# Longer rows for the loads, three stores for four, and a later release of the first store, in a streaming add and GELU kernel

## The chip, the cores and the metric

One core of one Trainium2 chip (each batch of runs on one chip, not always the same). The metric is the device time of one execution in microseconds (us). The kernel before took 121.92 us, median of three runs (121.77 to 122.04).

## The reference

Two float32 arrays of 1024 x 4096 are added, and the tanh form of GELU is taken of the sum:

```python
def reference(x, y):
    z = x + y
    return (0.5 * z * (1 + np.tanh(np.sqrt(2 / np.pi) * (z + 0.044715 * z ** 3)))).astype(np.float32)
```

That is 33.55 MB to load and 16.78 MB to store, with a dozen operations per element.

## The kernel before

Each of the 128 partitions owns 8 rows, so a flat row of 32,768 values. The work is cut into 16 chunks of 2048 columns. GELU is computed as z times a sigmoid: POOL adds x and y (DVE does it for chunk 0), ACT squares into PSUM, DVE does a multiply-add there, ACT takes the sigmoid, and DVE multiplies PSUM by z back into SBUF. All transfers are issued by SP, in this order, to one DMA queue; x is loaded straight into the buffer `zt`, which also takes the result; y has two buffers of 8192 columns, so the third block of y waits for the adds of the first. The stores wait for the multiplies of their chunks, and the first store for that of chunk `FIRST` as well.

```python
    YS = 8192
    CH = 2048
    PS = 2
    loads = [2048, 6144, 8192, 8192, 8192]
    FIRST = 8
    stores = [16384, 8192, 4096, 4096]
    # ... cut ...
    by_pool = set(range(1, C))
    # ... cut ...
    def store(i):
        a, b = sr[i]
        ins = nc.sync.dma_start(out=ov[:, a:b], in_=zt[:, a:b])
        if i == 0:
            tc.add_manual_dep(
                ins.ins,
                muls[FIRST].name,
                mybir.DependencyInfo(mybir.DependencyClass.Sync, mybir.DependencyReason.DATA),
                reason="the stores join the queue when the last load is nearly done",
            )
    # ... cut ...
    def mul(c):
        a, b = cr[c]
        muls[c] = nc.vector.tensor_mul(out=zt[:, a:b], in0=wt[c], in1=zt[:, a:b]).ins
```

## Time and profile before

| | before |
|---|---|
| time, three runs | 121.77 to 122.04 us |
| span of the profiled run | 119.75 us |
| DMA queue, share of 16 engines' span | 98.6% |
| DVE, POOL, ACT busy | 62%, 56%, 51% |
| first packet starts, last packet ends | 1.03 us, 119.19 us |
| first store issued | 76.44 us |

The queue's row is the one to read first: the DMA engines are busy for 98.6% of the span and the busiest compute engine for 62%, so the question is what is in the queue. The prediction shows the lines.

A *packet* is one record of the DMA's work in the trace (start, duration, bytes); here it is one row of a transfer in one partition. The *turn* is where a DMA engine passes from its last load packet to its first store packet. The *stall* is what load packets before the turn lasted over the median of their size (1213 ns for 32 KB), summed and divided by the 16 engines. Where single engines are told of, their chains were put together from the packets' times, since the records carry no engine number.

### The profile page before, as it was taken

The numbers are of one execution on the slowest core, as the hardware profiler recorded it, in microseconds if no ns is written. First come the engines' busy times: TensorE is split into PE (matmuls) and PEld (weight loads), VectorE is DVE, ScalarE is ACT, GpSimd is POOL, SyncE is SP. The second block draws the span as 40 slices with busy tenths as digits, with TensorE's granted clock in tenths as the row PEclk, the third lists the DMA queues.
The fourth block names the chain that finished last, engine by engine and source line by source line (L and its number), as shares of the span: only waits on it lengthen the run. The fifth ranks groups of instructions, "written<-read, shape, count | busy, mean of one in ns | idle before, by whom it ended". The sixth has DMA issues, their size and how long they took to land.

```text
span 119.8 us, 174 instructions
## 1 busy us (share of the span) xinstructions
DVE 73.7 (62%) x34; ACT 61.0 (51%) x34; POOL 67.5 (56%) x19
## 2 busy tenths in 40 slices
DVE  0053600004999970749999949999993999990000
ACT  4006000009779706197797668888819879800000
POOL 0000000699980199999869999939999990000000
DMA  6999999989898999989898989998899889999996
GB/s 186 421 487 402 476 435 394 514 361 493 383 493 383 438 438 394 482 361 514 350 525 350 525 350 493 383 525 350 350 613 438 350 350 427 449 405 405 427 432 257
DMA packets 2016, 50.33 MB, mean 420 GB/s; under 512 B 224, under 2 KB 224, under 8 KB 224
## 3 DMA queue, kind: packets, MB, share of 16 engines
q1 hardware_dynamic: 2016, 50.33, 98.6%
HBM read 33.55 MB, written 16.78 MB: 420 GB/s over the span
## 4 chain that ended last, share of the span: by engine, by line
DMA 50%; POOL 26%; POOLq 4%; DVE 4%; DVEq 2%; ACT 2%; SPq 1%; issue 0%
DMA y<-in_y_dram 50%; POOL z L145 26%; POOLq L215 4%; DVE w L156 2%; DVEq L215 2%; DVE z L165 2%; ACT w L150 2%; SPq L121 1%; SPq L128 1%; POOLq L145 0%
## 5 line engine op out<-in xcount | busy, mean ns | idle before, releaser
L145 POOL TENSOR_TENSOR z<-z,y 128x2048 f32<-128x2048 f32 x15 | 67.3, 4519 | 31.1 <-DMA y<-in_y_dram 31.1
L156 DVE SCALAR_TENSOR_TENSOR w<-w,z 128x2048 f32<-128x2048 f32 x16 | 36.7, 2296 | 26.4 <-ACT w L150 26.1
L150 ACT ACTIVATE w<-z 128x2048 f32<-128x2048 f32 x16 | 30.1, 1882 | 38.3 <-POOL z L145 29.3
L165 DVE TENSOR_TENSOR z<-w,z 128x2048 f32<-128x2048 f32 x16 | 35.8, 2281 | 0.0
L161 ACT ACTIVATE w<-w 128x2048 f32<-128x2048 f32 x16 | 29.7, 1855 | 4.4 <-DVE w L156 4.4
L145 DVE TENSOR_TENSOR z<-z,y 128x2048 f32<-128x2048 f32 x1 | 2.3, 2293 | 6.1 <-DMA y<-in_y_dram 6.1
L200 ACT ACT_TABLE_LOAD x1 | 1.3, 1283 | 1.3 <-PEq L232 1.3
L199 DVE MEMSET one<- 128x1 f32 x1 | 0.1, 59 | 1.3 <-PEq L232 1.3
L232 POOL MEMSET const-float32-0.0<- 128x1 f32 x1 | 0.1, 98 | 0.2 <-issue 0.2
L200 ACT ACTIVATE one<-one 128x1 f32<-128x1 f32 x1 | 0.2, 203 | 0.0
L232 POOL MEMSET const-bfloat16-1.0<- 128x1 bf16 x1 | 0.1, 101 | 0.0
L232 POOL MEMSET const-uint8-127<- 128x1 uint8 x1 | 0.1, 101 | 0.0
L232 POOL MEMSET const-float32-1.0<- 128x1 f32 x1 | 0.1, 98 | 0.0
## 6 DMA issues: line engine op xcount, KB each, us to landing
z<-in_x_dram SPq DMA_DIRECT2D x3, 4096.0 KB, 34.6
y<-in_y_dram SPq DMA_DIRECT2D x3, 4096.0 KB, 25.3
out_dram<-z SPq DMA_DIRECT2D x1, 4096.0 KB, 22.2
out_dram<-z SPq DMA_DIRECT2D x2, 2048.0 KB, 14.1
z<-in_x_dram SPq DMA_DIRECT2D x1, 3072.0 KB, 13.4
y<-in_y_dram SPq DMA_DIRECT2D x1, 3072.0 KB, 20.3
z<-in_x_dram SPq DMA_DIRECT2D x1, 1024.0 KB, 4.9
y<-in_y_dram SPq DMA_DIRECT2D x1, 1024.0 KB, 6.9
```

What stands on the lines that cost most here:

```text
L121: nc.sync.dma_start(out=zt[:, a:b], in_=xv[:, a:b])
L128: nc.sync.dma_start(out=yt[s][:, o : o + b - a], in_=yv[:, a:b])
L145: eng.tensor_add(out=zt[:, a:b], in0=zt[:, a:b], in1=yt[s][:, o : o + b - a])
L150: nc.scalar.activation(out=wt[c], in_=zt[:, a:b], func=act.Square, scale=root)
L156: nc.vector.scalar_tensor_tensor(out=wt[c], in0=wt[c], scalar=c1, in1=zt[:, a:b], op0=alu.add, op1=alu.mult)
L161: nc.scalar.activation(out=wt[c], in_=wt[c], func=act.Sigmoid)
L165: muls[c] = nc.vector.tensor_mul(out=zt[:, a:b], in0=wt[c], in1=zt[:, a:b]).ins
L199: nc.vector.memset(one, 0.0)
L200: nc.scalar.activation(out=one, in_=one, func=act.Sigmoid)
L215: tc.compile()
L232: nc = _bacc.Bacc("TRN2", target_bir_lowering=False, num_devices=1)
```

## The change

Fewer and longer transfers: eight loads of 32 KB rows in place of ten with 8, 24 and 32 KB; three stores in place of four. The first store is also issued later: it waits for the first half of chunk 9's multiply, not for all of chunk 8's.

```diff
-    loads = [2048, 6144, 8192, 8192, 8192]
-    FIRST = 8
-    stores = [16384, 8192, 4096, 4096]
+    loads = [8192, 8192, 8192, 8192]
+    FIRST = 9
+    stores = [16384, 10240, 6144]
@@
-        muls[c] = nc.vector.tensor_mul(out=zt[:, a:b], in0=wt[c], in1=zt[:, a:b]).ins
+        parts = 2 if c == FIRST else 1
+        n = (b - a) // parts
+        for o in range(0, b - a, n):
+            ins = nc.vector.tensor_mul(
+                out=zt[:, a + o : a + o + n],
+                in0=wt[c][:, o : o + n],
+                in1=zt[:, a + o : a + o + n],
+            )
+            muls.setdefault(c, ins.ins)
```

## The prediction

Where the text below told of the hardware what no trace or run of this case shows, the passage is cut and the place marked. The sum runs 121.92 - 0.23 - 0.1 = 121.6 us (121.59). These numbers stand as estimates:

- the gain of 0.1 us at the start, out of the 0.66 us of excess measured there;
- that DVE's and POOL's first adds, ready together, would run one after the other, so that POOL's would come later by the length of DVE's (2293 ns). The trace before does not show it, since its DVE add ran alone. Rival 1 is the opposite order: POOL's three adds first, DVE's after them;
- the first store at 77.4 us. From the trace alone: half of a multiply of 2.28 us from 76.33 gives 77.47, less the 0.2 us of earlier landings some 77.3;
- the 0.45 us after which the store's descriptors "should reach the engines": it is read off the start of the dent (76.44 to 76.89 us) alone, for the records hold packets and no descriptors. So is the latency of a first store in rival 3, read off the dent's 1.9 us.

> **What bounds the kernel now.** I read the page from the top: engine shares, the row of DMA slices, the queue, then the waits and the chain.
>
> ```profile
> span 119.8 us, 174 instructions
> DVE 73.7 (62%) x34; ACT 61.0 (51%) x34; POOL 67.5 (56%) x19
> ...
> q1 hardware_dynamic: 2016, 50.33, 98.6%
> HBM read 33.55 MB, written 16.78 MB: 420 GB/s over the span
> ```
>
> No compute engine is busy for two thirds of the span; the one DMA queue is busy for 98.6% of it. So the question is what the 16 DMA engines do in 119.75 us. Next the DMA in four stretches (columns: stretch and length, then DVE, ACT, POOL busy, clock, DMA share, GB/s):
>
> ```profile
> 0.00:3.00 3.00, 0.06 (x1) 1.49 (x2) 0.20 (x4) 1.00 0.67 188
> 3.00:76.00 73.00, 44.34 (x20) 37.04 (x20) 46.39 (x11) 1.00 1.01 436
> 76.00:80.00 4.00, 4.00 (x3) 3.03 (x3) 2.94 (x1) 1.00 0.99 369
> 80.00:119.75 39.75, 25.29 (x12) 19.46 (x11) 17.95 (x4) 1.00 0.96 414
> ```
>
> From 3 to 76 us the queue runs flat at 436 GB/s. (A packet's bytes count where it starts, so short windows swing.) It loses at the two ends and in a dent at 76 to 80 us, where the first store joins. The chain of waits says 50% "DMA y" and 26% POOL, and the DMA issues waited 46.4 us for the multiplies; but [...] the 98.6% says that the queue was full. The timeline dates the issues:
>
> ```profile
> 7.47 2.29 DVE L145 TENSOR_TENSOR z<-z,y 128x2048 f32<-128x2048 f32 x1 [6.08 <-DMA y<-in_y_dram]
> ...
> 22.12 13.45 POOL L145 TENSOR_TENSOR z<-z,y 128x2048 f32<-128x2048 f32 x3 [21.69 <-DMA y<-in_y_dram]
> ...
> 48.01 2.30 DVE L156 SCALAR_TENSOR_TENSOR w<-w,z 128x2048 f32<-128x2048 f32 x1 [3.81 <-ACT w L150]
> ...
> 74.13 4.48 DVE L165 TENSOR_TENSOR z<-w,z 128x2048 f32<-128x2048 f32 x2
> ...
> 76.44 31.41 SPq L132 DMA_DIRECT2D out_dram<-z  x4
> ```
>
> The two multiplies from 74.13 are those of chunks 8 and 9 (each 2.28 us); chunk 8's ends at 76.41 and releases the first store at 76.44.
>
> The trace keeps a record of each packet (start, duration, bytes); one row of a transfer is one packet. Median durations: 309 ns for 8 KB, 611 for 16 KB, 912 for 24 KB, 1213 for 32 KB, 2418 for 64 KB, 9 for the 4-byte packet that each engine ends a transfer with. From 8 to 64 KB that is 2109 ns for 57,344 bytes: 0.03678 ns per byte, or 27.19 GB/s per engine, and about 8 ns on top per packet. Now the sum for one of the 16 engines (8 rows of each transfer):
> - first packet at 1.03 us
> - packets at their medians: 16 of 8 KB 4.94, 16 of 24 KB 14.59, 56 of 32 KB 67.93, 8 of 64 KB 19.34, 16 of 16 KB 9.78, 14 end packets 0.13: 116.71 us
> - excess over the medians 1.34 us: 0.66 in packets that start between 1 and 2 us, 0.53 in those from 76 to 80 us, 0.15 scattered
> - last packet's end (119.19) to the end of the span: 0.56 us
>
> Sum 119.64 of 119.75 us. The measured time, 121.92, is 2.17 us more than the span. Nothing but bytes, packet ends, these excesses and the two fixed ends is in the time.
>
> [...] the one DVE add with two SBUF inputs ran alone at 7.47, and the others read one input from PSUM, beside which POOL's adds stay at 4493 to 4541 ns.
>
> **The change, part by part.**
> Fewer packets. The four small loads (8 and 24 KB rows) become two of 32 KB rows; the stores of 32, 16 and 16 KB rows become 40 and 24 KB. Per engine: 64 of 32 KB at 1213 = 77.63; 8 of 64 KB 19.34; 8 of 40 KB, by the line above 1514 each (an estimate), 12.11; 8 of 24 KB 7.30; 11 end packets 0.10. Sum 116.48 us against 116.71: **0.23 us saved**. All of it is on the path, since the queue is the path.
>
> Start. The first packet should still start near 1.03 us. The 0.66 us of excess there sits on the first packet or two of each engine. [...] I count a gain of 0.1, with 0 to 0.4 possible.
>
> The first add. The DVE add of chunk 0 now waits for all of y's first block, as POOL's add of chunk 1 does: both become ready at about 21.8 instead of 7.4 and 22.0. [...] In the trace DVE starts 0.10 us after the landing (7.37 to 7.47), POOL 0.14 us after (21.98 to 22.12), so DVE should win. Then POOL's three adds come 2.3 us later (end 37.9, not 35.57), y's third block is issued at 37.9 rather than 35.60, and the compute of block 0 ends some 2.3 us later. Neither is on the path: x's third block occupies the queue until 50.6, and DVE waited 3.81 us before its instruction at 48.01, which absorbs the shift. Cost 0. Without contention the chain keeps its times too, because before, too, chunk 0's second half waited for chunk 1 at 26.65.
>
> First store. [...] The store is issued at about 77.4, some 1.0 us later. The loads' last packets ended at 79.6 to 80.5; without the dent and with fewer packets they would end at about 78.9 to 79.7. The dent began 0.45 us after the issue (packets from 76.89), so the stores' descriptors should reach the engines at 77.85, still a packet ahead of the end: no bubble. The dent itself I take as the cost of the first store reaching the engines, and keep at 0.53, give or take 0.3.
>
> Later stores. 40 KB rows need the multiply of chunk 12, which ended at 96.3 by the chain; store 0 keeps the queue until 99.3 or later. 24 KB rows need chunk 15 (107.5); store 1 lasts until about 111.5. Margins 3 and 4 us: hidden.
>
> Split multiply: one more DVE instruction[...], on an engine with 38% idle: 0.
>
> Sum: 121.92 - 0.23 - 0.1 = **121.6 us**.
>
> **Rivals.**
> 1. The DVE add starves. [...] add 0 runs at 35.3 to 37.6, block 0 ends at 57.5 instead of 44.2, and with DVE working pairs of chunks in 9.0 us back to back, half of chunk 9 is done at 83.2. The queue runs dry from about 80 to 83.7: about 3.7 us, some 125.4 us. [...] against it: DVE's 0.04 us lead. I give it 5 to 6%.
> 2. The later store removes the dent, because it is caused by store and loads in flight together: 0.5 us less, 121.1. For it: packets are slow only there; against: 1 us later they still overlap.
> 3. The later store is too late: first-store latency falls into an empty queue. 0.3 to 0.6 us more: about 122.0. The dent's 1.9 us from 76.9 to 78.8 suggests that a first store takes time to get going.
>
> **Range and chances.** Rivals 2 and 3 are half a microsecond either side, and before's own three runs span 121.77 to 122.04. So 121.1 to 122.0 should hold it 8 times in 10. Faster by 2% is 119.5, below 1.03 + 116.48 + 0.56 + 2.17 = 120.24, which has no excess at all: 1%. Slower by 2% needs rival 1: 5%.
>
> **What would show it.** Right: 1584 packets, the queue again at 98% or more, a first store issued near 77.4, a dent of about 0.5 us just after it, store packets following loads without a gap, POOL's first adds later by 2.3 us with DVE's add at 21.9 unchanged. Wrong: DVE's add of chunk 0 lasting or starting far later than 22 and the first store after 80 (rival 1); a DMA gap at 79 to 81 us (rival 3); no slow packets there (rival 2); a first-packet excess far from 0.66 us.

## The result and the profile after

The changed kernel took **121.11 us** (median of six runs, 120.99 to 121.43), against 121.80 for the kernel before on the same chip (121.49 to 122.04, six runs). The ratio is 0.9947, with a 95% interval of 0.9929 to 0.9965. All ratios here are the mean time of one kernel's fast runs over that of the other's of the same rounds, so they are not quite the ratios of the medians. By the 2% rule that is "same"; the interval nevertheless excludes 1. The predicted 121.6 was 0.5 us too high.

The page of the changed kernel answers the four lines shown of before:

```profile
span 118.9 us, 170 instructions
DVE 73.7 (62%) x35; ACT 61.0 (51%) x34; POOL 69.7 (59%) x19
...
q1 hardware_dynamic: 1584, 50.33, 98.6%
HBM read 33.55 MB, written 16.78 MB: 423 GB/s over the span
```

It has 1584 packets and the same 98.6%: the queue is still the bound, and only POOL's busy time moved, by 2.2 us. Its DMA by stretches (columns as in the prediction):

```profile
0.00:3.00 3.00, 0.06 (x1) 1.49 (x2) 0.20 (x4) 1.00 0.81 262
3.00:76.00 73.00, 44.57 (x20) 37.15 (x20) 48.80 (x11) 1.00 1.01 435
76.00:80.00 4.00, 4.00 (x4) 3.16 (x2) 2.69 (x1) 1.00 1.22 524
```

The flat part is unchanged (435 against 436 GB/s). The dent is gone: 524 GB/s at 76 to 80 us, against 369. (Bytes count where a packet starts, and here the first 64 KB packets start inside the stretch. The packet records say it without that distortion: the load packets of before between 76 and 80 us had 0.53 us of excess per engine, those of after 0.00.) The timeline of the changed kernel:

```profile
21.84 2.29 DVE L145 TENSOR_TENSOR z<-z,y 128x2048 f32<-128x2048 f32 x1 [20.44 <-DMA y<-in_y_dram]
21.88 15.58 POOL L145 TENSOR_TENSOR z<-z,y 128x2048 f32<-128x2048 f32 x3 [21.44 <-DMA y<-in_y_dram]
...
47.78 2.30 DVE L156 SCALAR_TENSOR_TENSOR w<-w,z 128x2048 f32<-128x2048 f32 x1 [1.69 <-ACT w L150]
...
77.33 29.77 SPq L132 DMA_DIRECT2D out_dram<-z  x3
```

DVE's add and POOL's first add start 0.04 us apart, DVE first. DVE's takes its usual 2.29 us; POOL's three adds take 15.58 us, not 13.45. One group line of each kernel (POOL's adds: shortest, median, longest in ns) shows that a single instruction carries it, first before, then after:

```profile
L145 POOL TENSOR_TENSOR z<-z,y x15: 4493/4518/4541, 22.1 to 94.3; 128x2048 f32<-128x2048 f32 x15
```

```profile
L145 POOL TENSOR_TENSOR z<-z,y x15: 4508/4520/6622, 21.9 to 93.6; 128x2048 f32<-128x2048 f32 x15
```

POOL's first add lasted 2.1 us longer than its usual 4.5. DVE's idle time before its instruction near 48 us shrank from 3.81 to 1.69 us, which is where those 2.1 us ended.

Where the 0.84 us between the two profiled spans went, by the packet records: the 16 engines finished at 118.81 us on average before, and at 118.10 after, 0.71 less. Of this 0.53 is the stall, 0.06 the start (0.66 to 0.60), and 0.12 the rest, mostly the packets saved. The span waits for the slowest engine, and the stall had hit the engines unequally (0.11 to 0.83 us each): the last engine finished 0.38 us behind the mean before, and 0.16 after, 0.22 less. Against it the time from the last packet to the end of the span grew from 0.56 to 0.65. In all 0.71 + 0.22 - 0.09 = 0.84.

So most of the gain is the vanished stall, and the prediction had kept it. Did the later release remove it, or the rows, or chance?

### The profile page after: what moved, and what is told of

The parts are those of the page before. It is cut to its first block, busy times and chain, and to the rows that moved or that the text cites. A ratio compares the mean times of both kernels' runs of the same rounds, so it can differ in the third digit from the quotient of the medians.

```text
span 118.9 us, 170 instructions
## 1 busy us (share of the span) xinstructions
DVE 73.7 (62%) x35; ACT 61.0 (51%) x34; POOL 69.7 (59%) x19
## 2 busy tenths in 40 slices
DMA packets 1584, 50.33 MB, mean 423 GB/s; under 512 B 176, under 2 KB 176, under 8 KB 176
## 3 DMA queue, kind: packets, MB, share of 16 engines
q1 hardware_dynamic: 1584, 50.33, 98.6%
## 4 chain that ended last, share of the span: by engine, by line
DMA 51%; POOL 26%; POOLq 4%; DVE 4%; DVEq 2%; ACT 2%; issue 0%; SPq 0%
DMA y<-in_y_dram 51%; POOL z L145 26%; POOLq L223 4%; DVE w L156 2%; DVEq L223 2%; DVE z L168 2%; ACT w L150 2%; SPq L121 0%; POOLq L145 0%
## 5 line engine op out<-in xcount | busy, mean ns | idle before, releaser
L145 POOL TENSOR_TENSOR z<-z,y 128x2048 f32<-128x2048 f32 x15 | 69.4, 4661 | 28.2 <-DMA y<-in_y_dram 28.2
L168 DVE TENSOR_TENSOR z<-w,z 128x2048 f32<-128x2048 f32 (+1 forms) x17 | 35.9, 2155 | 0.0
L145 DVE TENSOR_TENSOR z<-z,y 128x2048 f32<-128x2048 f32 x1 | 2.3, 2292 | 20.4 <-DMA y<-in_y_dram 20.4
```

Of the source, the lines that this page charges most:

```text
L145: eng.tensor_add(out=zt[:, a:b], in0=zt[:, a:b], in1=yt[s][:, o : o + b - a])
L168: ins = nc.vector.tensor_mul(out=zt[:, a + o : a + o + n], in0=wt[c][:, o : o + n], in1=zt[:, a + o : a + o + n],)
```

## The experiments

Theory A: the stall comes from the first store joining the queue too far ahead of the turn; as I first put it, the stall was to come at the moment of joining. Rival B: it belonged to the old rows, or was chance. Rival C: it falls where the queue turns, however early the store joined. Rivals D and E are about how often it is paid: once, by the first store of the program (D), or at every turn (E). All twelve runs gave correct results; each has a profile. Each time is the median of six executions (e7: four), and a stall is that of the one profiled. The kernel before was timed in each batch.

| run | first store issued, us | stall 76-80 us, us | median, us (range) | ratio to before |
|---|---|---|---|---|
| before, first batch | 76.44 | 0.53 | 121.80 (121.49-122.04) | 1 |
| changed kernel | 77.33 | 0.00 | 121.11 (120.99-121.43) | 0.9947 |
| e1: changed, FIRST 8 | 76.45 | 0.56 | 121.56 (121.37-121.92) | 0.9993 |
| e2: before, half of 9 | 77.38 | 0.01 | 121.22 (121.18-121.46) | 0.9969 |
| e3: new loads alone | 76.15 | 0.22 | 121.52 (121.36-121.98) | 0.9993 |
| e4: new stores alone | 76.53 | 0.04 | 121.54 (121.33-122.04) | 0.9995 |
| e5: changed, whole of 9 | 78.48 | 0.03 | 121.23 (121.11-121.29) | 0.9964 |
| e6: changed, FIRST 7 | 67.94 | 0.74 | 121.99 (121.91-122.11) | 1.0028 |
| e7: changed, late | 80.62 | 0, then a gap of 2.17 | 123.26 (123.23-123.30) | 1.0132 |
| e8: early small store | 35.02 and 79.88 | 1.08 at 47-51 | 122.37 (122.17-122.56) | 1.0056 |
| e9: e8, FIRST 7 | 34.99 and 67.93 | 1.05 at 47-51 | 122.57 (122.39-122.72) | 1.0083 |
| e10: changed again | 77.26 | 0.00 | 121.12 (121.08-121.34) | 0.9967 |
| e11: changed, 8 KB stores | 77.33 | 0.00 | 121.92 (121.70-122.05) | 1.0029 |
| e12: changed, half of 8 | 75.29 | 0.90 | 121.83 (121.68-122.17) | 1.0027 |

The 95% intervals are some 0.002 to 0.0026 either way. In the three later batches the kernel before had medians of 121.55 (121.36 to 122.01), 121.58 (121.33 to 122.13) and 121.45 us (121.33 to 122.26), 11 runs each.

### The change in its parts (e1 to e4)

**e1**, the changed kernel with the old release:

```diff
-    FIRST = 9
+    FIRST = 8
-        parts = 2 if c == FIRST else 1
+        parts = 1
```

> The changed kernel with the first store released by chunk 8's whole multiply again (about 76.2 us). Theory A (the dent comes with the early join, about two packets ahead of the last load's end): slow packets with 0.4 to 0.6 us of excess per engine return between 76 and 80 us, time about 0.5 us over the changed kernel, ratio to before about 0.999. Rival B (the dent was chance, or belonged to the old row lengths): no excess there, ratio about 0.995 as the whole change.

The stall was back at 0.56 us and the ratio was 0.9993, as theory A had it; rival B's 0.995 lies outside the interval (0.9973 to 1.0013).

**e2**, the kernel before with only the release moved:

```diff
-    FIRST = 8
+    FIRST = 9
```
(with the multiply of chunk 9 in two halves, as in the change)

> The kernel before with only the release of the first store moved to half of chunk 9's multiply. Theory A: no slow packets at 76 to 80 us, ratio to before about 0.996 (0.5 us less). Rival B: the dent stays or the ratio is 1.000.

The stall was gone, the ratio 0.9969 (0.9952 to 0.9986). So the release alone, on the old rows, gives a gain that no other part does.

**e3** and **e4**, the rows alone:

```diff
-    loads = [2048, 6144, 8192, 8192, 8192]
+    loads = [8192, 8192, 8192, 8192]
```

> The kernel before with the eight loads of 32 KB rows alone. Both theories: 16 data packets and 2 end packets fewer per engine, by 8 to 9 ns each 0.15 us, and perhaps 0.06 us at the start: ratio about 0.998. POOL's three first adds last 15.6 us in place of 13.45. Theory A: the dent of some 0.5 us is there; rival B has it gone if the old loads' rows made it (ratio 0.994).

```diff
-    stores = [16384, 8192, 4096, 4096]
+    stores = [16384, 10240, 6144]
```

> The kernel before with only the stores of 64, 40 and 24 KB rows. Both: 8 data packets and 1 end packet fewer per engine, 0.07 us: ratio about 0.999 to 1.000. Theory A: the dent is there. Rival B as chance: there or not.

Ratios of 0.9993 and 0.9995, neither distinguishable from 1, nor from the 0.998 and 0.999 expected. But the stall was 0.22 us in one profile and 0.04 in the other, with the same release as before. So with a release by chunk 8 the stall is not a fixed 0.53: over the four profiled runs of that kind it was 0.04 to 0.56. It goes along with the times: the two with the full stall took 121.92 us each, the other two 121.42 and 121.36. This would also explain why all kernels with this release spread so much, 121.33 to 122.26 for the kernel before over its 39 runs, while the 18 runs with a release at half of chunk 9 (the change, e2, e10) lie between 120.99 and 121.46.

### The place and the price of the join (e5 to e7, e12)

**e5** releases by the whole of chunk 9's multiply (1.15 us later), **e6** by chunk 7's (9.4 us earlier), **e12** by the first half of chunk 8's (2.0 us earlier), each on the changed kernel:

```diff
-        parts = 2 if c == FIRST else 1
+        parts = 1                          # e5, with FIRST = 9
```

> The changed kernel with chunk 9's multiply whole, so that the first store is issued at about 78.35 us, 1.0 us later. [...] Theory A (early join stalls engines, later is as good until the queue runs dry): no slow packets, no gap, ratio 0.995 as the changed kernel. Rival (the half multiply was needed, the store is already late by then): gap after the loads of 0.3 us or more, ratio 0.998 or more.

```diff
-    FIRST = 9
+    FIRST = 7                              # e6, with parts = 1
```

> The changed kernel with the first store released by chunk 7's multiply, the last it reads, at about 67.8 us, some 9 load packets per engine ahead of the loads' end. Theory A as a stall at the moment of joining: slow packets within 2.5 us of 68.2, up to 0.8 us in an engine, ratio about 0.997 to 1.000. Rival C (the stall belongs to the queue's turn from loads to stores near 77 to 79 us, and the join merely must not fall there): no slow packets at 68 to 71 us, ratio 0.995 or a dent at 77 to 79 us.

```diff
-    FIRST = 9
+    FIRST = 8                              # e12, parts as in the change
```

> The changed kernel with the first store released by half of chunk 8's multiply, about 75.1 us. With the join at 67.9 us every engine stalled and the six runs lay within 0.2 us at 121.99; with the joins at 76.2 to 76.5 us the stall was between 0.04 and 0.63 us and the runs spread over 0.6 us. If there is a threshold near there: a full stall of 0.6 us or more, runs close together, ratio 1.002 to 1.004. If the stall is merely chance with any early join: a spread as wide as with chunk 8, ratio about 0.999.

The stretches of e6 show when the stall comes:

```profile
68.00:70.00 2.00, 2.00 (x1) 0.20 (x1) 2.00 (x2) 1.00 1.22 524
70.00:72.00 2.00, 0.41 (x2) 2.00 (x2) 2.00 (x1) 1.00 0.76 328
72.00:74.00 2.00, 2.00 (x2) 1.44 (x1) 2.00 (x1) 1.00 1.06 459
74.00:76.00 2.00, 2.00 (x2) 1.86 (x1) 2.00 (x2) 1.00 1.22 524
76.00:78.00 2.00, 2.00 (x2) 1.71 (x1) 2.00 (x1) 1.00 0.83 262
78.00:80.00 2.00, 2.00 (x2) 1.43 (x2) 0.71 (x1) 1.00 0.91 328
```

From 68 to 76 us, right after the store was issued at 67.94, the mean of the four stretches is 459 GB/s, as in the changed kernel, where no store was queued yet; the swings are those of start times. At 76 to 80 us there are 295. By the records, all packets from 68 to 76 us were within 8 ns of the median; then the last two load packets of each engine took 1258 to 1947 ns instead of 1213. So theory A holds in that the early join is what costs, and rival C holds for the place: **an early join costs nothing when it happens; the stall comes in the last two load packets before the turn.** (By the chains, nearly all of it can lie in the last packet but one: on average 895 ns there and 1 in the last in e12, 558 and 1 in e1, 441 and 303 in e6.) My first form of theory A fell here.

The further ahead, the surer: 0.74 and 0.90 us with joins at 67.94 and 75.29, 0.04 to 0.56 with joins from 76.15 to 76.53, and 0.03 or less from 77.26 on. (e6's six runs all took 121.91 us or more; e12's profiled run was the slowest of its six, so its 0.90 is likely above what is usual there.) The window of e12 beside that of e10, the changed kernel in the same batch:

```profile
76.00:80.00 4.00, 4.00 (x3) 3.04 (x3) 2.85 (x1) 1.00 0.85 270
```

```profile
76.00:80.00 4.00, 4.00 (x4) 3.23 (x2) 2.62 (x1) 1.00 1.22 524
```

My expectation that e12's runs would lie close together missed: they span 0.5 us. e5 agrees with theory A: no stall at the turn, no gap, 0.9964. The packets of e5's profiled run had 0.30 us of small excesses between 3 and 76 us, against 0.10 in the changed kernel and 0.20 in e1; I do not explain them.

**e7** releases the first store by the multiply-add of chunk 10, after the loads' end:

```diff
-    FIRST = 9
+    FIRST = 10                             # parts = 1
-                muls[FIRST].name,
+                stts[FIRST].name,          # the multiply-adds, recorded in the same way
```

> The changed kernel with the first store released by the middle multiply-add of chunk 10, at about 80.7 us, after the loads' last packet (79.2 to 79.6). Both theories: a gap of the DMA of about 1.6 to 2.2 us (80.7 plus 0.45 us, plus a first-packet latency of up to 0.6 us as at the start, less 79.4), ratio about 1.008 to 1.013. It says what a late store costs against an early one, and whether a first store into an empty queue has a slow first packet.

```profile
78.00:79.00 1.00, 1.00 (x2) 0.42 (x2) 0.71 (x1) 1.00 0.99 426
79.00:80.00 1.00, 1.00 (x1) 1.00 (x1) 0.00 (x0) 1.00 0.01 0
80.00:81.00 1.00, 0.94 (x2) 1.00 (x2) 0.82 (x1) 1.00 0.00 0
81.00:82.00 1.00, 1.00 (x1) 1.00 (x1) 1.00 (x1) 1.00 2.46 1049
```

Between 79 and 81 us no data packet starts: the loads had ended at 79.0 to 79.6, the store was issued at 80.62, and its first packet began at 81.47, 0.85 us after the issue began (the expectation's 0.45 us, and up to 0.6 more, were estimates from the dent of before and from the excess at the start). The engines stood idle for 2.17 us on average, and the kernel was 2.1 us slower than the changed one (123.26 against 121.12 to 121.23). Those first store packets took 2448 to 2462 ns, only some 35 ns over the usual 2418. So here a late store cost its lateness in full, 1.26 us from the loads' mean end (79.36) to the issue, and 0.91 us more until the engines' first store packets began (81.53 on average).

### The first store, or every turn (e8, e9)

**e8** stores chunk 0 by itself early, between the third block's x and y loads, and the rest (56 KB rows) with chunk 8's multiply:

```diff
-    stores = [16384, 10240, 6144]
+    stores = [2048, 14336, 10240, 6144]
-    FIRST = 9
+    FIRST = 8                              # for store 1; parts = 1
-        sp += [(load_x, i), (load_y, i)]
+        sp += [(load_x, i)] + [(store, 0)] * (i == 2) + [(load_y, i)]
```

> The changed kernel with chunk 0 stored by itself between the third block's x and y loads (issued near 35 us, queued behind some 13 packets per engine), and the rest of the first store (56 KB rows) released by chunk 8's whole multiply as in the kernel before, near 76.3 us. Theory D (the stall is a cost of the very first store, paid once): slow packets near 35.5 us and none at 76 to 79; ratio about 0.999. Theory A: slow packets at 76 to 79 us again, up to 0.8 us in an engine, whatever was stored before; ratio 0.998 to 1.001. The 9 extra packets per engine are 0.09 us by their 8 to 9 ns.

The early store was queued some 12 packets ahead and its turn, at 51 us, stalled by 1.08 us per engine. The stretch around it, first in the changed kernel, then in e8:

```profile
46.00:52.00 6.00, 2.39 (x2) 3.41 (x2) 6.00 (x2) 1.00 1.01 437
```

```profile
46.00:52.00 6.00, 2.44 (x2) 3.41 (x2) 6.00 (x2) 1.00 0.92 318
```

It moved 318 GB/s in place of 437. The second turn, at 83 us, had no slow packet. As a test it was spoiled: everything ran some 3.5 us later than I had allowed for, because the small store and its stall came ahead of y's third block, and chunk 8's multiply ended at 79.85 us. The main store joined only 2.7 to 3.4 us ahead of the turn, as near as in the kernel before, where a stall is uncertain anyway. My expected place of the first stall, near 35.5 us, was a miss, as was the expected ratio of at most 1.001; it was 1.0056: the stall was twice the size that I had reckoned with, and the later compute left a gap of 0.39 us per engine before the third store.

**e9** mends it, with the main store released by chunk 7's multiply:

```diff
-    FIRST = 8
+    FIRST = 7
```

> The kernel with chunk 0 stored early, but the rest of the first store released by chunk 7's multiply (some 71 us in its later timeline), so that it joins many load packets ahead of the second turn from loads to stores (near 82 us). The turn at 51 us should stall about 1 us per engine again in the last two load packets, as it did (mean 1.06). Theory D (only the first store of the program pays): none at the second turn, time as with the late join of that kernel, ratio 1.0055. Theory E (each turn for which the store is queued well ahead pays): 0.5 to 1.0 us more in the last two load packets before the second turn, ratio 1.009 to 1.014.

Now the main store was issued at 67.93 us, 15 us ahead of its turn, further than in e6. The first turn stalled again (1.05 us), the second did not: between 78 and 83 us the packets had 0.01 us of excess per engine on average, and 0.14 us in the worst engine. The stretches of e9 show both turns, with 324 GB/s on average from 46 to 52 us and 592 from 79 to 83, where the first 56 KB packets start:

```profile
46.00:48.00 2.00, 0.32 (x2) 1.76 (x1) 2.00 (x1) 1.00 1.35 492
48.00:50.00 2.00, 2.00 (x1) 0.00 (x0) 2.00 (x1) 1.00 0.99 295
50.00:52.00 2.00, 0.09 (x1) 1.65 (x1) 2.00 (x2) 1.00 0.44 184
79.00:81.00 2.00, 2.00 (x2) 1.61 (x2) 2.00 (x1) 1.00 1.14 492
81.00:83.00 2.00, 2.00 (x2) 1.42 (x2) 1.21 (x1) 1.00 1.61 692
```

So in this profile rival D holds and E falls: **only the program's first store pays.** The ratio, 1.0083, lies between what the two theories expected. Its interval, 1.0058 to 1.0109, just misses D's 1.0055 and takes in the low end of E's 1.009 to 1.014, so by the time alone E would be the nearer. The packet records decide. Of the 1.40 us by which e9's profiled span exceeds e10's, the first turn's stall (1.05) and a gap of 0.32 us per engine before the third store make up nearly all (smaller terms cancel), which leaves no room for a second stall of 0.5 us; and part of the difference from D's ratio, that of e8, is the kernel before, whose median was 0.13 us lower in this batch.

### The control and the rows (e10, e11)

**e10** is the changed kernel, without an edit.

> The changed kernel itself, as the neighbour of the other three on the same chip: ratio 0.995 again, no stall at the turn near 79 us. If the good join were luck in the first profile, this one shows a stall of 0.2 us or more, or a ratio over 0.998.

No stall again; median 121.12, as the first time (121.11). The ratio is 0.9967 (0.9945 to 0.9989), a little above the expected 0.995, which the interval takes in: here the kernel before had a median of 121.45 rather than 121.80, as in the two batches before. By the medians the change gained 0.7 us in the first batch and 0.3 in this one. That this follows how often the kernel before stalls fits its spread, but is not shown: only one of its runs was profiled, and the batches ran on different chips.

**e11** cuts the stores of the changed kernel to 8 KB rows, to enlarge the cost of a packet:

```diff
-    stores = [16384, 10240, 6144]
+    stores = [2048] * 16
```

> The changed kernel with its stores cut into 16 of 8 KB rows; join at half of chunk 9 as there. 128 store packets of 309 ns per engine (39.55 us) in place of 8 of 2418, 8 of 1514 and 8 of 912 (38.75 us), and 13 more end packets of 9 ns: 0.92 us more than the changed kernel by the packet sum, so ratio to before about 1.0025. If rows cost more than their packets show (gaps between transfers, waits for issue), the ratio is 1.006 or more; if less, 0.998 or below.

Measured: 121.92 against 121.12 us for e10 beside it, 0.80 us for 104 more data packets and 13 more end packets per engine; ratio 1.0029, expected 1.0025. The 16 engines ended 0.70 us later on average. That is under the sum of 0.92: consecutive packets of one engine overlap by 3 to 4 ns in the records, which is 0.36 us more in e11 than in e10, so each adds about 4 to 5 ns and not 8. This would make 0.56 us; most of the other 0.14 is excess of the small store packets over their own median (0.12 us). At 4.5 ns the 24 data packets and 3 end packets that the change saves come to some 0.13 us (24 x 4.5 ns plus 3 x 6 ns, an estimate). The 0.10 us between the medians of e2 (121.22) and of the changed kernel (121.12) fits it, though they are of different batches and the intervals of both are wider.

No version beat the changed kernel: among the joins tried, 77.3 us is within the good window, 78.5 is not better.

## Why the prediction was right or wrong

It was right in its range and its class: 121.11 us in 121.1 to 122.0, and "same". That the range held it by 0.01 us is in part luck: its lower end was drawn for rival 2, while the middle, 121.6, rests on a step that failed. By its own steps:

1. *The queue is the path.* Right: 98.6% before and after, 1584 packets as said, and compute shifts of 2 us changed nothing. That its sum for the kernel before closed to 0.11 us is partly luck, though. It lays the packets of an average engine end to end, while they overlap by 0.44 us in all; and it ends with the last engine, which was 0.38 us behind the mean. The two nearly cancel.
2. *Fewer packets, 0.23 us.* The mechanism is right, the size about twice too large. The packets' durations add up as predicted, but they overlap by 3 to 4 ns; 0.10 to 0.13 us remain (e2, e11).
3. *The start, 0.1 us.* Measured 0.06 in the profiled pair, and 0.51 to 0.71 us of excess over all runs with either row length: no effect of the rows that rises above that scatter.
4. *The first add.* Right: DVE started 0.04 us ahead and kept its 2.29 us; POOL came 2.13 us later (2.3 predicted); y's third block was issued at 37.48 us (37.9 predicted, which left out that POOL would start 0.24 us earlier); DVE's wait near 48 us took it up. Rival 1, the starving DVE add, did not occur. In this trace the add that started first lost nothing (2292 ns, 2293 alone in the kernel before), and the other took about that much longer (6622 ns; the shortest of POOL's 15 adds took 4508). What happens when POOL's starts first it does not show.
5. *The first store.* The issue time (77.4 predicted, 77.33 measured) and "no bubble" were right. **The step that failed is "The dent itself I take as the cost of the first store reaching the engines, and keep at 0.53, give or take 0.3".** It is a cost of the first store, as e9 shows, but not one that is always paid: with the store joining one or two packets ahead of the turn it is nothing (0.00 to 0.01 us: the changed kernel twice, e2, e11), with a join far ahead it is 0.7 to 1.1 us. The prediction's reading of the waits, that a store issued behind a full queue costs nothing, failed with it: e6's store was issued 9.4 us earlier than the changed kernel's, behind a full queue, and the kernel took 0.87 us more. Rival 2, no dent and 121.1 us, is what happened; to the tenth by luck, since it counted from 121.92, and the kernel before took 121.80 beside the changed one. Its reason, that store and loads are in flight together, was too coarse: in e6 the store was queued behind the loads for 8 us that ran at full speed.
6. *One number for before.* I took the one profiled run of before, with a stall of 0.53 us, for the kernel. With this release the stall varies from run to run, and the kernel before also has runs of 121.33 us.

What stays open: why a first store that is queued far ahead slows the last two load packets, when the same store, joining later, makes the turn at full speed. The trace gives each packet's start and duration and nothing of what an engine waits for within it. Nor did any run show what decides between a small and a full stall at 76.2 to 76.5 us.

## What to carry to other kernels

Where one DMA queue is full from end to end, look at its packets one by one around each change of direction; a mean over the span (98.6% in both kernels) hides half a microsecond there. Let the first store join when only a packet or two per engine are left ahead of it: that stalled by 0.00 to 0.03 us here, earlier cost up to 0.9 us (1.1 with an early small store), and a store issued after the loads' end cost the whole lateness and some 0.9 us more. And before a change of half a per cent is explained from one profile, see how much the kernel before varies by itself, and which of its terms vary.
